# Stick-breaking scans over 640 columns in two pieces, and weight copies ranked 40 instructions higher

## The chip, the cores and the metric

The kernel runs on one core of a Trainium2 chip. The metric is the device time of one execution in microseconds (us). Engines: TensorE (PE) multiplies and transposes, VectorE (DVE) and ScalarE (ACT) evacuate and compute, GpSimd (POOL) does elementwise work on SBUF, SyncE (SP) issues nearly all DMAs.

## The reference, cut to what matters

One decoder layer over 1024 positions of width 1024, in float32. The projection `h @ w_in` feeds 8 heads of forgetting attention and 8 heads of stick-breaking attention (head width 64); then come group norms, an output projection, and a gated MLP with a causal convolution. The change concerns the stick-breaking heads, and one step that both kinds of heads share:

```python
mask = kpos[None, :] < qpos[:, None]
z = jnp.einsum('bhqd,bhkd->bhqk', qi, kf) * scale
log_beta = jax.nn.log_sigmoid(z)
log_one_minus = jnp.where(mask, jax.nn.log_sigmoid(-z), 0.0)
after = lax.cumsum(log_one_minus, axis=3, reverse=True) - log_one_minus
weights = jnp.where(mask, jnp.exp(log_beta + after), 0.0)
out = jnp.einsum('bhqk,bhkd->bhqd', weights, vf)
```

So a weight is sigmoid(z) times the product of sigmoid(-z) over all later keys before the query.

## The kernel before, in words

Queries are handled in blocks of 128 (`i` = 0 to 7); block `i` sees n = 128 (i + 1) keys, so its widest row has 128 to 1024 columns. Blocks go in groups of two (`g` = 0 to 3), in the order 0, 1, 3, 2, for one head after another: 8 forgetting heads, then 8 stick-breaking ones.

For a stick-breaking block, `score` (lines 455 to 501) multiplies q with the keys (lines 472, 473; keys come as a high and a low part), adds the mask (476), and lets ACT write sigmoid(-z) to `qi` and sigmoid(z) to `w` (486, 487), in up to two chunks. Then DVE runs one scan (line 499), backwards from column T - 1 = 1023 over n columns: a running product, in place. Column T of `qi` holds 1.0. POOL multiplies `w` with the scanned row, shifted by one column (line 500). There are two `qi` tiles and four `w` tiles.

`trans` (503 to 521) turns the weights of a group: PE transposes up to four 128x128 tiles into one PSUM bank `tp` (511; two banks), ACT copies the bank to `ph` (519), rounded to the matmul type, and DVE subtracts, `pl` = `tp` - `ph` (520), the low part. On the diagonal the tiles are `pth` and `ptl`, of 384 columns. `pv` (523 to 541) multiplies them with v: lines 531 (`ph`) and 532 (`pl`), into the bank `o`; then DVE folds `o` into `ot` (`tm`, 540 and 541).

Between these steps runs filler work that needs no attention result: projections of later heads (lines 164 to 166, 282 to 284, evacuated by lines 237 to 242 and 291 to 293), and in the last heads the output projection of the forgetting group, with `ogl` (624), `t` (657, 658) and its store (659). SP loads the next head's q, `kh`, `kl` and v (437 to 450).

The order on PE, DVE, ACT and POOL is made by a planner: it lays out the whole program by modelled times, and where several instructions of an engine are ready takes that with the lowest rank number, which is the place in the program. `tc.high_priority(offset=n)` gives the instructions inside a rank n places earlier (a negative n: later). Each engine then runs its list in order. SP's list is in program order. `GIVE = 60` is such an offset already, for POOL's weight splits. The forget gate's cumulated sum (line 334) is a scan in two chained pieces already.

Of the kernel before, what the change touches and what calls it, by code (L numbers as in the profile page):

```python
# [13 lines left out]
ALU = mybir.AluOpType  # L14
# [5 lines left out]
T = 1024  # L20
# [34 lines left out]
UA = 3  # L55

GIVE = 60

PARTS = ((0, 512), (512, 256), (768, 256))
NORM_AT = ((1, 3), (2, 3), (3, 0))  # L60
# [5 lines left out]
def f32(ap):  # L66
    return ap.bitcast(F32)
# [3 lines left out]
def layer(ctx, tc, xT, wqk, wv0, wv, wout, wup, wdn, cols, fbias, yT):  # L71
    nc = tc.nc
# [43 lines left out]
    class W:  # L116
# [16 lines left out]
        def split(self, upto):  # L133
# [4 lines left out]
            while self.done < upto:  # L138
                q = self.n // self.pieces
                sl = slice(self.done * q, (self.done + 1) * q)  # L140
                first = self.act or self.index < 2
                with tc.high_priority(offset=0 if first else -GIVE):
                    if first:
# [273 lines left out]
    def defer(n, f):  # L417
        pend.append([n, f])
# [36 lines left out]
    def score(p, hb, i, ws):  # L455
        fox = p < NFOX
        q, kh, kl, vt, fbt = heads[p, hb]
        n = (i + 1) * P
        w = pp.tile([P, T], F32, name="w")
        ws[i] = w  # L460
        m = None
        if not fox:
            if len(qi) < NQ:
                qi.append(own.tile([P, T + 1], F32, name=f"qi{len(qi)}"))
                nc.gpsimd.memset(qi[-1][:, T:T + 1], 1.0)
            qt = qi[count[0] % NQ]
            count[0] += 1
        for c0, cn in CHUNKS[i]:
            s = ps_s.tile([P, 512], F32, name="s")
            qb = q[:, i * P:(i + 1) * P]  # L470
            diag = c0 <= i * P < c0 + cn
            nc.tensor.matmul(s[:, :cn], qb, kh[:, c0:c0 + cn], start=True, stop=False)
            nc.tensor.matmul(s[:, :cn], qb, kl[:, c0:c0 + cn], start=False, stop=not diag)
            if diag:
                o = i * P - c0
                nc.tensor.matmul(s[:, o:o + P], identb, mask_f if fox else mask_s,  # L476
                                 start=False, stop=True)
            un = min(cn, n - c0)
            if fox:
                m2 = small.tile([P, 1], F32, name="m")  # L480
                nc.vector.tensor_tensor_reduce(  # L481
                    out=w[:, c0:c0 + un], in0=s[:, :un], in1=fbt[:, c0:c0 + un], scale=-1.0,
                    scalar=3.0e38 if m is None else m, op0=ALU.add, op1=ALU.min, accum_out=m2)
                m = m2
            else:
                act(qt[:, T - n + c0:T - n + c0 + un], s[:, :un], AF.Sigmoid, scale=-1.0)  # L486
                act(w[:, c0:c0 + un], s[:, :un], AF.Sigmoid)

        if fox:
            l = small.tile([P, 1], F32, name="l")  # L490
            act(w[:, :n], w[:, :n], AF.Exp, scale=-1.0, bias=m, accum_out=l)  # L491

            def rest():
                nc.vector.reciprocal(l, l)  # L494
                nc.gpsimd.tensor_scalar(w[:, :n], w[:, :n], l, 1.0, ALU.mult, ALU.mult)  # L495
        else:
            def rest():
                rev = slice(T - 1, T - n - 1 if n < T else None, -1)
                nc.vector.tensor_tensor_scan(qt[:, rev], qt[:, rev], qt[:, rev], 1.0, ALU.mult, ALU.bypass)  # L499
                nc.gpsimd.tensor_tensor(w[:, :n], w[:, :n], qt[:, T - n + 1:T + 1], ALU.mult)  # L500
        defer(0, rest)

    def trans(g, mm, ws, box):
        last = mm == g
        z = P if last else 0
        tp = ps_t.tile([P, 512], F32, name="tp")
        for a, kb in enumerate((2 * mm + 1, 2 * mm)):
            for b in range(2):
                if kb > 2 * g + b:
                    continue  # L510
                nc.tensor.transpose(tp[:, a * 256 + b * P:a * 256 + (b + 1) * P],  # L511
                                    ws[2 * g + b][:, kb * P:(kb + 1) * P], ident)
        if last:
            ph, pl = ptl[count[1] % 2]
            count[1] += 1
        else:
            ph = ptp.tile([P, 512], F32R, name="ph")
            pl = ptp.tile([P, 512], F32R, name="pl")
        nc.scalar.copy(ph[:, z:], tp[:, z:])  # L519
        nc.vector.tensor_tensor(pl[:, z:], tp[:, z:], f32(ph[:, z:]), ALU.subtract)  # L520
        box[mm] = (ph, pl)

    def pv(p, hb, g, mm, box):
# [20 lines left out]
    def finish(p):  # L544
# [3 lines left out]
        def go():  # L548
# [9 lines left out]
            eng = nc.vector if p == NPAIR - 1 else nc.gpsimd  # L558
            with tc.high_priority(offset=0 if p == NPAIR - 1 else -GIVE):
                for sl in (slice(0, 512), slice(512, T)):  # L560
# [12 lines left out]
    def attention_stream():  # L573
        hs = [(p, hb) for p in range(NPAIR) for hb in range(2)]
        prev = []
        yield 0, partial(load_v, 0, 0)
        for n, (p, hb) in enumerate(hs):
            ws = {}
            order = ORDER_LAST if n == len(hs) - 1 else ORDER
            for gi, g in enumerate(order):  # L580
                if gi == 1 and n + 1 < len(hs):
                    yield 0, partial(load_head, *hs[n + 1])
                    yield 0, partial(load_v, *hs[n + 1])
                for i in (2 * g, 2 * g + 1):
                    cost = 2 * sum(c for _, c in CHUNKS[i]) / 2400 + 0.06
                    yield cost, partial(score, p, hb, i, ws)
                yield from prev
                box = {}
                tr = [(TRC, partial(trans, g, mm, ws, box)) for mm in range(g + 1)]
                pvs = [(0.67 - TRC, partial(pv, p, hb, g, mm, box)) for mm in range(g + 1)]  # L590
                prev = tr[:LAG]
                for mm in range(g + 1):
                    prev.append(pvs[mm])
                    prev += tr[mm + LAG:mm + LAG + 1]
                if n == len(hs) - 1:
                    if gi == 1:
                        prev += [(0, partial(load_og, 4)), (0, partial(load_og, 5))]
                    if gi == 2:
                        prev += [(0, partial(load_og, 6))]
            if hb == 1:  # L600
                prev.append((0.4, partial(finish, p)))
        yield from prev
# [683 lines left out]
```

## Time and profile before

| | |
|---|---|
| median of 3 runs | 1420.33 us (1416.86 to 1420.97) |
| profiled execution | 1420.63 us |
| its span | 1418.8 us |
| PE busy in the span | 1306.7 us (92%) |
| DVE busy | 1113.8 us (79%) |
| ACT busy | 622.8 us (44%) |
| POOL busy | 759.5 us (54%) |
| scans of line 499 on DVE | 64, 104.0 us |
| copies of line 519 on ACT | 160 |
| subtractions of line 520 on DVE | 160 |

The span is what the profiler saw from the first to the last instruction; the execution's own time is a little longer. "Busy" is the time in which an engine worked on an instruction, not the time in which it set the end.

### The profile page before, as it was taken

The page shows a single profiled execution, that of the slowest core. Times are in us where ns is not written, and L with a number is a line of the kernel's source. Part 1 is how long each engine was busy: PE and PEld are TensorE (multiplying, and loading weights), DVE is VectorE, ACT ScalarE, POOL GpSimd, SP SyncE. Part 2 cuts the span into 40 slices and gives each one's busy share as a digit, 9 for nine tenths or more (in the row PEclk, how much of TensorE's full clock was granted, in tenths as well). Part 3 has the DMA queues.
Part 4 walks back from the last instruction along what each step waited for, and adds up shares of the span by engine and source line. Part 5 has one row for each costly group of instructions (what it writes and reads, how often), then busy time and mean ns, then how long its engine had stood idle before and what let it go on. Part 6 is the DMA issues. An engine that isn't in the chain of part 4 may idle for free.

```text
span 1418.8 us, 19128 instructions
## 1 busy us (share of the span) xinstructions
PE 1306.7 (92%) x6640; PEld 1074.8 (76%) x6640; DVE 1113.8 (79%) x1646; ACT 622.8 (44%) x1136; POOL 759.5 (54%) x664
## 2 busy tenths in 40 slices
PE   7899999999898887799889999999999988999895
PEld 6879878877787766678667788888888866878685
DVE  7346555655676678697999999999889899899987
ACT  6234434444454455354544444344343363344334
POOL 4254354444647584440005788887778864445413
PEclk9999999999999999999989999999999999999997
DMA  5656555544534455547512332233332265445313
GB/s 182 193 159 193 149 164 157 147 134 133 165 105 133 119 155 157 149 157 237 184 60 68 111 111 95 92 111 112 111 112 97 97 222 193 163 149 169 99 30 119
DMA packets 97233, 194.89 MB, mean 137 GB/s; under 512 B 8680, under 2 KB 35688, under 8 KB 97136
## 3 DMA queue, kind: packets, MB, share of 16 engines
q1 hardware_dynamic: 96272, 193.04, 43.5%
q8 instruction: 52, 0.85, 0.3%
q10 hardware_dynamic: 864, 0.64, 0.1%
q14 instruction: 45, 0.37, 0.1%
HBM read 132.79 MB, written 60.85 MB: 136 GB/s over the span
## 4 chain that ended last, share of the span: by engine, by line
PE 53%; DMA 17%; DVE 16%; POOL 6%; issue 4%; ACT 2%; SPq 2%; DVEq 0%; POOLq 0%; ACTq 0%
PE u L165 8%; PE u L166 8%; PE u L164 8%; PE pj L164 5%; PE pj L166 5%; PE pj L165 5%; DMA q<-qkd 4%; DVE qi L499 3%; DMA vd<-vs 2%; PE tp L511 2%; PE o L532 2%; DMA oraw<-od 2%; PE pj L282 1%; PE pj L284 1%; PE pj L283 1%
## 5 line engine op out<-in xcount | busy, mean ns | idle before, releaser
L886 POOL TENSOR_TENSOR s<-wraw 128x512 f32<-128x512 f32 (+1 forms) x32 | 52.7, 1647 | 210.7 <-DMA wraw<-in_wup_dram 145.5
L500 POOL TENSOR_TENSOR w<-w,qi 128x128 f32<-128x128 f32 (+3 forms) x64 | 94.2, 1482 | 79.9 <-DVE qi L499 41.8
L913 ACT CAST wh<-s 128x512 fp32r<-128x512 f32 (+1 forms) x136 | 79.4, 591 | 119.9 <-POOL s L887 68.7
L499 DVE TENSOR_TENSOR_SCAN qi<-qi 128x128 f32<-128x128 f32 (+3 forms) x64 | 104.0, 1633 | 27.7 <-ACT qi L486 24.9
L146 POOL TENSOR_SCALAR wh<-wraw 128x256 fp32r<-128x256 f32 (+1 forms) x104 | 51.3, 512 | 124.4 <-DMA wraw<-in_wv_dram 51.0
L511 PE MATMUL tp<-ident,w 128*128 128x128 f32 x576 | 94.4, 282 | 19.3 <-DVE pl L520 8.4
L164 PE MATMUL pj<-xh,wh 128*128 128x512 f32 x224 | 101.8, 454 | 3.2 <-DVE yf L298 3.2
L511 PEld LDWEIGHTS tp<-ident,w 128*128 128x128 f32 x576 | 71.1, 145 | 38.2 <-DVE pl L520 12.0
L915 POOL TENSOR_TENSOR wl<-wraw,wh 128x512 fp32r<-128x512 f32 x58 | 100.0, 1731 | 0.0
L520 DVE TENSOR_TENSOR pl<-tp,ph 128x512 fp32r<-128x512 f32 x96 | 65.0, 685 | 36.1 <-ACT ph L519 35.8
L166 PE MATMUL pj<-xh,wl 128*128 128x512 f32 x224 | 90.9, 406 | 0.0
L491 ACT ACTIVATE w<-w,m 128x128 f32<-128x128 f32 (+3 forms) x64 | 49.7, 776 | 92.5 <-DVE m L481 87.2
L165 PE MATMUL pj<-xl,wh 128*128 128x512 f32 x224 | 90.1, 402 | 0.0
L1012 DVE SCALAR_TENSOR_TENSOR tg<-ua,col,tg 128x1023 f32<-128x1023 f32 (+1 forms) x44 | 88.9, 2020 | 0.2 <-ACT tg L1010 0.2
L486 ACT ACTIVATE qi<-s 128x512 f32<-128x512 f32 (+2 forms) x96 | 47.5, 494 | 86.7 <-PE s L476 41.0
L913 ACT CAST wh<-wraw 128x512 fp32r<-128x512 f32 (+1 forms) x96 | 55.1, 590 | 67.6 <-DMA wraw<-in_wdn_dram 26.3
L495 POOL TENSOR_SCALAR w<-w,l 128x128 f32<-128x128 f32 (+3 forms) x64 | 47.9, 754 | 68.0 <-DVE l L494 35.1
L282 PE MATMUL pj<-wh,xh 128*128 128x256 f32 (+1 forms) x256 | 78.5, 307 | 1.5 <-DVE yf L298 1.5
L519 ACT CAST ph<-tp 128x512 fp32r<-128x512 f32 x96 | 55.9, 588 | 52.8 <-PE o L531 33.1
L915 POOL TENSOR_TENSOR wl<-s,wh 128x512 fp32r<-128x512 f32 x44 | 73.1, 1662 | 10.8 <-ACT wh L913 10.4
L148 POOL TENSOR_TENSOR wl<-wraw,wh 128x256 fp32r<-128x256 f32 (+1 forms) x104 | 78.0, 772 | 0.2
L1012 DVE SCALAR_TENSOR_TENSOR tv<-ub,col,tv 128x1023 f32<-128x1023 f32 (+1 forms) x44 | 73.9, 1680 | 2.3 <-ACT tv L1010 2.1
(366 smaller groups left out, 4508.6 us busy)
## 6 DMA issues: line engine op xcount, KB each, us to landing
wraw<-in_wup_dram SPq DMA_DIRECT2D x47, 512.0 KB, 3.7
st<-td SPq DMA_DIRECT2D x74, 256.0 KB, 3.9
qkd<-hl SPq DMA_DIRECT2D x32, 512.0 KB, 3.0
td<-tg SPq DMA_DIRECT2D x44, 256.0 KB, 2.3
vd<-vs SPq DMA_DIRECT2D x32, 256.0 KB, 4.5
q<-qkd SPq DMA_DIRECT2D x16, 512.0 KB
kh<-qkd SPq DMA_DIRECT2D x32, 256.0 KB, 17.0
kl<-qkd SPq DMA_DIRECT2D x32, 256.0 KB, 17.5
```

The lines of the kernel that those rows point to most:

```text
L148: eng.tensor_tensor(self.lo[:, sl], self.raw[:, sl], f32(self.hi[:, sl]), ALU.subtract)
L164: nc.tensor.matmul(ps, ah, bh, start=start, stop=False)
L165: nc.tensor.matmul(ps, ah, bl, start=False, stop=False)
L166: nc.tensor.matmul(ps, al, bh, start=False, stop=stop)
L282: nc.tensor.matmul(ps[:, :n], xh[k][:, sl], h, start=(k == 0), stop=False)
L499: nc.vector.tensor_tensor_scan(qt[:, rev], qt[:, rev], qt[:, rev], 1.0, ALU.mult, ALU.bypass)
L500: nc.gpsimd.tensor_tensor(w[:, :n], w[:, :n], qt[:, T - n + 1:T + 1], ALU.mult)
L511: nc.tensor.transpose(tp[:, a * 256 + b * P:a * 256 + (b + 1) * P], ws[2 * g + b][:, kb * P:(kb + 1) * P], ident)
L520: nc.vector.tensor_tensor(pl[:, z:], tp[:, z:], f32(ph[:, z:]), ALU.subtract)
L913: nc.scalar.copy(h[:, o:o + w], src)
L915: eng.tensor_tensor(l[:, o:o + w], src, f32(h[:, o:o + w]), ALU.subtract)
L1012: nc.vector.scalar_tensor_tensor(t[:, s:], us[:, :T - s], col[:, cw + tap:cw + tap + 1], t[:, s:], op0=ALU.mult, op1=ALU.add)
```

## The change

Two edits, in the functions printed above.

The scan of a block with n over 640 (blocks 5, 6 and 7) is made in two instructions: the last 512 columns, then the other n - 512 (256, 384 or 512). The second starts from the last value of the first, read from `qi`.

The copy to `ph` (or `pth`) on ACT and the subtraction to `pl` (or `ptl`) on DVE get a rank 40 places earlier, in all 16 heads.

```diff
 GIVE = 60
+
+SOON = 40
...
         else:
             def rest():
-                rev = slice(T - 1, T - n - 1 if n < T else None, -1)
-                nc.vector.tensor_tensor_scan(qt[:, rev], qt[:, rev], qt[:, rev], 1.0, ALU.mult, ALU.bypass)
+                last = 1.0
+                for a, b in ((T, T - 512), (T - 512, T - n)) if n > 640 else ((T, T - n),):
+                    rev = slice(a - 1, b - 1 if b else None, -1)
+                    nc.vector.tensor_tensor_scan(qt[:, rev], qt[:, rev], qt[:, rev], last, ALU.mult, ALU.bypass)
+                    last = qt[:, b:b + 1]
                 nc.gpsimd.tensor_tensor(w[:, :n], w[:, :n], qt[:, T - n + 1:T + 1], ALU.mult)
         defer(0, rest)
...
-        nc.scalar.copy(ph[:, z:], tp[:, z:])
-        nc.vector.tensor_tensor(pl[:, z:], tp[:, z:], f32(ph[:, z:]), ALU.subtract)
+        with tc.high_priority(offset=SOON):
+            nc.scalar.copy(ph[:, z:], tp[:, z:])
+            nc.vector.tensor_tensor(pl[:, z:], tp[:, z:], f32(ph[:, z:]), ALU.subtract)
         box[mm] = (ph, pl)
```

## Rows read from the trace of the kernel before

**Rows 1.** Stretches: start:end, length, busy PE, PEld, DVE, ACT, POOL, granted clock, DMA, GB/s.
```profile
98.00:345.00 247.00, 236.55 (x1529) 204.19 (x1529) 147.65 (x429) 108.17 (x234) 111.56 (x160) 0.99 0.54 155
345.00:645.00 300.00, 260.42 (x1520) 215.93 (x1520) 221.59 (x284) 147.25 (x312) 171.77 (x161) 0.94 0.48 140
```

**Rows 2.** Waits of PE from 345 to 645: total us, times, longest.
```profile
PE o L532 <- DVE pl L520: 12.1, 7, 3.2
PE tp L511 <- POOL w L500: 7.7, 5, 5.4
...
PE tp L511 <- DVE pl L520: 4.8, 3, 2.0
PE o L532 <- DVE ptl L520: 4.0, 6, 1.9
```

**Rows 3.** Timeline of one head: start, duration, instruction [idle before <-releaser].
```profile
401.44 1.78 POOL L500 TENSOR_TENSOR w<-w,qi 128x896 f32<-128x896 f32 x1 [3.11 <-DVE qi L499]
...
402.19 3.17 DVE L499 TENSOR_TENSOR_SCAN qi<-qi 128x1024 f32<-128x1024 f32 x1 [0.92 <-ACT qi L486]
...
403.03 0.59 ACT L519 CAST ph<-tp 128x512 fp32r<-128x512 f32 x1
...
405.39 0.61 DVE L293 SCALAR_TENSOR_TENSOR vs<-pj,rst,vs 128x128 fp32r<-128x128 f32 x2
...
405.92 0.68 DVE L520 TENSOR_TENSOR pl<-tp,ph 128x512 fp32r<-128x512 f32 x1
...
406.65 0.38 PE L532 MATMUL o<-pl,vt 128*128 128x256 f32 x1 [1.78 <-DVE pl L520]
```

**Rows 4.** Timeline: short scans of three widths.
```profile
413.44 1.76 DVE L499 TENSOR_TENSOR_SCAN qi<-qi 128x768 f32<-128x768 f32 x1 [0.87 <-ACT qi L486]
...
510.71 2.28 DVE L499 TENSOR_TENSOR_SCAN qi<-qi 128x1024 f32<-128x1024 f32 x1
...
611.37 1.21 DVE L499 TENSOR_TENSOR_SCAN qi<-qi 128x512 f32<-128x512 f32 x1
```

**Rows 5.** Timeline of PE: gaps that end with a low copy.
```profile
372.30 0.39 PE L532 MATMUL o<-pl,vt 128*128 128x256 f32 x1 [0.98 <-DVE pl L520]
...
442.47 0.39 PE L532 MATMUL o<-pl,vt 128*128 128x256 f32 x1 [2.21 <-DVE pl L520]
...
478.49 0.39 PE L532 MATMUL o<-pl,vt 128*128 128x256 f32 x1 [3.22 <-DVE pl L520]
...
621.57 0.38 PE L532 MATMUL o<-pl,vt 128*128 128x256 f32 x1 [0.93 <-DVE pl L520]
...
632.19 0.66 PE L511 MATMUL tp<-ident,w 128*128 128x128 f32 x4 [2.03 <-DVE pl L520]
```

**Rows 6.** Timeline of DVE ahead of the last of these.
```profile
630.28 1.25 DVE L624 SCALAR_TENSOR_TENSOR ogl<-oraw,col,ogh 128x1024 fp32r<-128x1024 f32 x1
...
631.46 0.68 DVE L520 TENSOR_TENSOR pl<-tp,ph 128x512 fp32r<-128x512 f32 x1
```

**Rows 7.** Timeline of PE: two other gaps late in the stretch.
```profile
549.41 0.35 PE L472 MATMUL s<-kh,q 128*128 128x256 f32 x1 [1.45 <-DMA kh<-qkd]
...
593.77 0.80 PE L164 MATMUL pj<-ogh,wh 128*128 128x512 f32 x1 [5.43 <-DVE t L657]
```

**Rows 8.** Timeline: one product on POOL and the transposes that read it.
```profile
443.37 2.00 POOL L500 TENSOR_TENSOR w<-w,qi 128x1024 f32<-128x1024 f32 x1
...
446.32 0.60 PE L511 MATMUL tp<-ident,w 128*128 128x128 f32 x4
```

**Rows 9.** Busy time by stretch, behind two of the gaps (columns as above).
```profile
406.60:412.60 6.00, 5.95 (x34) 5.71 (x35) 3.41 (x6) 2.52 (x7) 2.19 (x2) 0.72 0.37 126
442.40:448.40 6.00, 5.93 (x36) 5.15 (x37) 4.46 (x7) 4.05 (x10) 4.43 (x4) 1.00 0.33 126
```

**Rows 10.** Waits from 345 to 640, all engines: one row.
```profile
ACT ph L519 <- PE o L531: 21.1, 7, 10.3
```

**Rows 11.** Timeline of POOL: the product of another head's block 6.
```profile
369.48 3.75 POOL L500 TENSOR_TENSOR w<-w,qi 128x896 f32<-128x896 f32 x1
```

## The prediction

> **What bounds the kernel now.** I read the busy time by stretch first. In the forgetting-attention stretch (98 to 345 us) TensorE (PE) is busy 236.55 of 247.00 us, so nearly nothing is to be won there. In the stick-breaking stretch (345 to 645 us) it is busy 260.42 of 300.00 us at a mean granted clock of 0.94: 39.6 us are idle, and all scans of the change lie here [rows 1]. Then I read what PE waited for in this stretch. 20.9 us of the idle time end with a `pl` or `ptl` copy of line 520: 12.1 us in seven gaps before the second attention product (line 532), 4.8 us in three gaps before a transpose, 4.0 us in six gaps on `ptl`. POOL's product of line 500 ends another 7.7 us [rows 2].
>
> The timeline of one such gap shows why `pl` is late. The scan of 1024 columns starts at 402.19 and takes 3.17 us. `ph` is ready at 403.03 + 0.59 = 403.62, but VectorE (DVE) works in order: the scan, two `vs` evacuations, then `pl` at 405.92. PE, which needs `pl`, stands for 1.78 us until 406.65 [rows 3]. Of the seven gaps of 12.1 us I list five, each behind the 1024-column scan of a different head: 0.98, 1.78, 2.21, 3.22 and 0.93 us [rows 3, 5]. The same rows show what stretches a scan. A 1024-column scan can take 2.28 us [rows 4]; this one began while POOL's product (401.44 to 403.22) ran, and it ended 2.14 us after the product did. So it seems to have stood still until POOL was done.
>
> **What the split gives.** Each head has three scans over 640 columns (blocks 5, 6 and 7), and there are 8 stick-breaking heads: 24 scans become 48. A 512-column scan takes 1.21 us, a 1024 one 2.28, a 768 one 1.76 [rows 4]. Two pieces of 512 are 2.42 us, so a split costs about 0.15 us of DVE: 24 x 0.15 = 3.6 us. This is hidden: DVE is busy 221.59 of 300.00 us in the stretch [rows 1]; if that cover were gone, the 3.6 us would be the price. What comes back: after the first piece DVE can take `pl`, which is then 2.28 - 1.21 = 1.07 us earlier behind a 1024 scan and 1.76 - 1.21 = 0.55 us earlier behind a 768 one. A `pl` that outranks its neighbours by 40 also passes the small work that stood before it.
>
> Gap by gap, never more than the gap itself:
> - 372.30: the whole 0.98. 442.47: 1.07 of 2.21. 478.49: 1.07 of 3.22. 621.57: the whole 0.93 [rows 5].
> - 406.65: 1.07, and the first of the two `vs` evacuations and a part of the second, 0.53 (405.92 - 405.39), so 1.60 of 1.78 [rows 3].
> - The other two of the seven hold 12.1 - 9.1 = 3.0 us. I count them as nothing: some microseconds behind the one PE waits for the DMA of `kh` (549.41), behind the other for 5.43 us for an evacuation that a store holds up (593.77); arriving there earlier only lengthens those waits [rows 7].
> - The three gaps before a transpose hang on 768 scans: 0.55 each, and at 632.19 also the `ogl` of 1.25 us that stands ahead of `pl` [rows 5, 6]: 2 x 0.55 + 1.80 = 2.90.
> - The six `ptl` gaps stand behind 512 and shorter scans, which stay whole. Only the rank could help: between 0 and 4.0 us [rows 2]. I take 0, the nearest row being an undivided scan.
>
> Sum: 0.98 + 1.60 + 1.07 + 1.07 + 0.93 + 2.90 = 8.55 us.
>
> **What is late next.** The second piece now waits for `pl` (0.68 us) and often `ptl`, so the product of block 7 on POOL, and the transposes that read it, come about 1.3 us later, while PE arrives 1 us sooner. PE bears that where it has over 2.3 us between product and transpose. At one head the product ends at 443.37 + 2.00 = 445.37 and the transpose starts at 446.32, a margin of 0.95 [rows 8]: up to 1.4 us of a new wait. But POOL also gets its turn between the pieces, so it starts the product of block 6 sooner. I take 0.5 us for this head, nothing at the others, and keep -1.4 us each for the five heads (7 us) as the bad end.
>
> **The clock.** After the gap of 1.78 us PE ran the next 6 us at a mean granted clock of 0.72, part of the time thus at the lower of its two levels (1.2 and 2.4 GHz); after the longer one of 2.21 us it kept 1.00 [rows 9]. So a gap doesn't always cost clock. The first of these shrinks to 0.2 us; I count its 6 x 0.28 = 1.7 us as won, and no other.
>
> **The rank in the forgetting heads.** There is no scan, but `ph` and `pl` move up against the exponentials and minima. The most that could come back is the 10.45 us that PE stands idle there. The other way: 8 heads x 4 groups x one cast of 0.59 us [rows 3] = 19 us of delays, of which PE, idle 4% of the time, would feel 0.8. I take 0.
>
> No DMA and no step of SP is moved; the bytes stay.
>
> **Sum.** 8.55 - 0.5 + 1.7 = 9.75 us. The profiled execution took 1420.63 us (span 1418.8 and 1.83 around it), 0.3 above the median of the runs. 1420.63 - 9.75 = 1410.9, so 1411 us.
>
> **The rivals.**
> *A: the rank does more than the split.* Where `ph` is done before the 1024 scan starts, the planner can put `pl` ahead of the whole scan, and `ptl` ahead of the 512 ones. Then all 20.9 us go, and the clock's 1.7: 1420.6 - 22.6 = 1398. For it: the gap of 3.22 us is longer than any scan of 2.28, so something was ready long before. Against it: at 402.19 `ph` ended 1.4 us after the scan began [rows 3], and an order that keeps DVE idle for a copy is not what a rank gives. 0.12.
>
> *B: nothing reaches the end.* The copies stay where they are in DVE's order, or the time won falls into the next waits: POOL's product (7.7 us in five gaps now [rows 2]), loads, stores [rows 7]. 1420 us. For it: the longest of PE's waits in rows 7 ends with an evacuation behind a store. Against it: over half of PE's 39.6 idle us end with `pl` or `ptl` [rows 1, 2], and their cause is the order on one engine. 0.20.
>
> *C, slower: POOL slips in between the pieces.* The product of block 6 at 369.48 took 3.75 us where the same shape takes 1.78 [rows 3, 11]: it waited for the scan to end. If the scan is cut and the two pieces still stand together in DVE's order, the waiting product starts after the first piece, the second piece waits for its 1.78 us, and everything behind it on DVE (`pl`, `tm`, evacuations) is that much later. For five gaps (four 1024 scans and one 768 one) 5 x 1.78 = 8.9 us: 1429.5 us. It decides only where `pl` is not between the pieces and a POOL instruction waits at that moment. Against it: `pl` outranks the second piece and takes just that place, and it has only one SBUF operand. 0.10. The Trainium skill ("SBUF — State Buffer", section "Who interferes with whom") has this as a rule: a VectorE instruction with two SBUF inputs and a GpSimd instruction that reads SBUF exclude one another, and the later one waits for the whole of the earlier. The trace agrees in both directions (2.14 us after the product's end; 3.75 for 1.78 us).
>
> *D, slower: ScalarE (ACT) is held.* ACT waited 21.1 us, seven times, with a `ph` at its head whose buffer PE had not yet read out [rows 10]. A `ph` ranked higher can come to stand ahead of the next block's sigmoids; they wait with it, the score banks fill up and PE stops. 3.0 us (21.1 / 7) in each of 8 heads is 24 us, less the 9.75 won: 1435 us. It decides where the hold is longer than the filler products that PE has before its next score. Against it: PE waits for ACT hardly at all now. 0.06.
>
> **Chances and range.** Forecast 0.52, with its own range 1404 to 1417; A 0.12; B 0.20; C 0.10; D 0.06. Within 0.3% (4.3 us, what a measurement of this kernel can tell from no change) lie 0.08 of the forecast and 0.14 of B: 0.22. Faster: 0.44 + 0.12 + 0.02 = 0.58. Slower: C, D and 0.04 of B: 0.20. The range goes from A's 1398 to 1430, past C; it leaves out D and the tails.
>
> **What would show it.** Right: in DVE's timeline of each stick-breaking head, scan piece, `pl`, scan piece; the 12.1 and 4.8 us of PE's waits for `pl` down to some 5 and 2; the stretch after 345 shorter by about 10 us, with the forgetting stretch and everything behind 645 as long as before. A would show `pl` before the first piece and the `ptl` waits gone too. C would show second pieces of 2.5 us or more with a POOL product inside them. D would show PE waiting for ACT's sigmoids in scores. I am wrong if the waits for `pl` fall and POOL's product (line 500) takes their place as what PE's transposes wait for, or if the stretch from 98 to 345 changes by more than 4 us.

## The result and the profile after

The changed kernel took 1426.67 us (median of 5 runs, 1424.61 to 1430.04), the kernel before 1417.97 beside it (5 runs, 1415.24 to 1420.97): a ratio of 1.0064 [1.0048, 1.008], 8.7 us slower. The forecast was 1411. The likely case went the wrong way, and the signs that the prediction gave for rival C are in the profile after.

First the stretches, as in [rows 1].

```profile
98.00:345.00 247.00, 235.16 (x1527) 201.88 (x1526) 148.46 (x430) 108.14 (x233) 111.19 (x160) 1.00 0.54 156
345.00:645.00 300.00, 254.56 (x1463) 210.41 (x1462) 224.55 (x292) 143.34 (x307) 164.59 (x161) 0.93 0.46 136
```

The forgetting heads are as before (PE's first wait behind them ends at 343.85 us instead of 344.25). In the second stretch PE is busy for 5.86 us less, at a clock lower by 0.01. A stretch of fixed length hides how late the work ends, so the next rows go from 344 us to the first matmul of `u`, the product that follows all heads (655.76 us before, 665.42 after): one row of the kernel before, then one of the kernel after.

```profile
344.00:655.76 311.76, 271.20 (x1579) 225.01 (x1580) 227.86 (x298) 152.21 (x319) 171.77 (x161) 0.95 0.47 140
```

```profile
344.00:665.42 321.42, 274.82 (x1579) 227.35 (x1580) 241.00 (x322) 152.04 (x319) 164.59 (x161) 0.94 0.46 135
```

The head stretch is 9.66 us longer, the whole span 9.1 (1427.9 against 1418.8): it all happens here. DVE has 24 instructions more and 13.1 us more busy time. Of PE's 9.66 us, 6.0 are idle time (40.6 to 46.6, length less busy). PE's busy time grew by 3.6; by windows of 5 us, busy time times (1 - granted clock) went from 12.9 to 16.2, so 3.3 of those 3.6 are time at the lower clock level.

What PE waited for, from 345 to 655 us (answers to [rows 2]; before, that window gives the same figures as the rows there):

```profile
PE o L538 <- DVE pl L526: 14.5, 6, 3.8
PE tp L516 <- DVE pl L526: 8.7, 7, 2.8
PE tp L516 <- POOL w L505: 8.3, 7, 4.0
PE o L538 <- DVE ptl L526: 4.4, 7, 2.0
```

The waits for `pl` rose from 12.1 + 4.8 to 14.5 + 8.7: 6.3 us, about the whole of the added idle time. The change was to shorten just these.

The first stick-breaking head shows how (timeline of DVE, POOL and PE; it answers to the first of [rows 5], a gap of 0.98 us):

```profile
369.41 1.19 DVE L503 TENSOR_TENSOR_SCAN qi<-qi 128x512 f32<-128x512 f32 x1
...
369.66 2.52 POOL L505 TENSOR_TENSOR w<-w,qi 128x896 f32<-128x896 f32 x1 [0.98 <-DVE qi L503]
...
370.64 2.62 DVE L503 TENSOR_TENSOR_SCAN qi<-qi 128x512 f32<-128x512 f32 x1
...
373.18 0.66 DVE L526 TENSOR_TENSOR pl<-tp,ph 128x512 fp32r<-128x512 f32 x1
...
373.89 0.39 PE L538 MATMUL o<-pl,vt 128*128 128x256 f32 x1 [1.73 <-DVE pl L526]
```

The two pieces of the 1024-column scan follow one another, `pl` behind both. POOL's product of block 6 was issued at 369.66, during the first piece; it ended at 372.18. The second piece took 2.62 us, where the first took 1.19, and ended at 373.26, 1.08 us after the product. So POOL got in between and the second piece stood until POOL was done: a slip, in what follows. PE's gap is 1.73 instead of 0.98. In the third head it is worse (the four pieces of blocks 6 and 7 in one row, with two POOL instructions inside it; 2.21 before [rows 5]):

```profile
437.18 7.24 DVE L503 TENSOR_TENSOR_SCAN qi<-qi 128x512 f32<-128x512 f32 x4 [1.87 <-ACT qi L488]
...
437.63 2.21 POOL L244 TENSOR_TENSOR hl<-full,hl 128x512 fp32r<-128x512 f32 x1
...
440.83 2.51 POOL L505 TENSOR_TENSOR w<-w,qi 128x896 f32<-128x896 f32 x1 [0.99 <-DVE qi L503]
...
444.34 0.66 DVE L526 TENSOR_TENSOR pl<-tp,ph 128x512 fp32r<-128x512 f32 x1
...
445.06 0.58 PE L538 MATMUL o<-pl,vt 128*128 128x256 f32 x1 [3.83 <-DVE pl L526]
```

In DVE's timeline of the eight heads `pl` stands between the pieces of the 1024-column scan in none (between those of the 768-column scan it does in the third, seventh and eighth). In five heads (1, 2, 3, 5, 7) the pieces stand together ahead of it; in the sixth and eighth something else parts them, and POOL slips in there too. The sixth head:

```profile
548.48 2.51 POOL L505 TENSOR_TENSOR w<-w,qi 128x896 f32<-128x896 f32 x1 [4.79 <-DVE qi L503]
...
549.46 0.42 DVE L546 COPY tm<-o 64x256 f32<-64x256 f32 x1
549.91 2.17 DVE L503 TENSOR_TENSOR_SCAN qi<-qi 128x512 f32<-128x512 f32 x1
```

So block 6's product slips into the 1024-column scan in four heads, the first, third, sixth and eighth: second pieces of 2.62, 2.61, 2.17 and 2.01 us where undisturbed ones take 1.27 to 1.28, in all 4.3 us more. In the second, fourth and seventh head the product began before the first piece, which stood for it (2.34 to 2.52 us), as the whole scan did before. In the fourth `pl` stands ahead of both pieces, and there the gap of 3.22 us [rows 5] is gone, but a new one of 2.01 us appears, on `ptl`, which a POOL product made late:

```profile
477.95 0.69 DVE L526 TENSOR_TENSOR pl<-tp,ph 128x512 fp32r<-128x512 f32 x1
478.09 1.78 POOL L505 TENSOR_TENSOR w<-w,qi 128x896 f32<-128x896 f32 x1 [2.31 <-ACT pth L525]
478.56 2.39 DVE L503 TENSOR_TENSOR_SCAN qi<-qi 128x512 f32<-128x512 f32 x1
480.87 0.53 DVE L526 TENSOR_TENSOR ptl<-tp,pth 128x384 fp32r<-128x384 f32 x1
481.32 1.27 DVE L503 TENSOR_TENSOR_SCAN qi<-qi 128x512 f32<-128x512 f32 x1
481.45 0.38 PE L538 MATMUL o<-ptl,vt 128*128 128x256 f32 x1 [2.01 <-DVE ptl L526]
```

### The profile page after: what moved, and what is told of

Same layout as the page of the kernel before. It is cut to its first block, busy times and chain, and to the rows that moved or that the text cites. A ratio compares the mean times of both kernels' runs of the same rounds, so it can differ in the third digit from the quotient of the medians.

```text
span 1427.9 us, 19139 instructions
## 1 busy us (share of the span) xinstructions
PE 1311.8 (92%) x6640; PEld 1076.5 (75%) x6640; DVE 1123.9 (79%) x1670; ACT 622.9 (44%) x1136; POOL 751.1 (53%) x664
## 4 chain that ended last, share of the span: by engine, by line
PE 53%; DVE 18%; DMA 16%; POOL 5%; issue 4%; ACT 3%; SPq 1%; DVEq 0%; POOLq 0%; ACTq 0%
PE u L167 8%; PE u L168 8%; PE u L166 8%; PE pj L168 5%; PE pj L166 5%; PE pj L167 5%; DVE qi L503 3%; DMA kl<-qkd 2%; DMA kh<-qkd 2%; DMA q<-qkd 2%; DMA wraw<-in_wqk_dram 2%; PE tp L516 2%; PE o L538 2%; DMA st<-td 2%; DVE wl L921 1%
## 5 line engine op out<-in xcount | busy, mean ns | idle before, releaser
L503 DVE TENSOR_TENSOR_SCAN qi<-qi 128x512 f32<-128x512 f32 (+4 forms) x88 | 115.4, 1317 | 25.7 <-ACT qi L488 22.2
L505 POOL TENSOR_TENSOR w<-w,qi 128x128 f32<-128x128 f32 (+3 forms) x64 | 87.4, 1371 | 88.4 <-DVE qi L503 53.4
L150 POOL TENSOR_TENSOR wl<-wraw,wh 128x256 fp32r<-128x256 f32 (+1 forms) x104 | 82.9, 816 | 0.5
```

Of the source, the lines that this page charges most:

```text
L150: eng.tensor_tensor(self.lo[:, sl], self.raw[:, sl], f32(self.hi[:, sl]), ALU.subtract)
```

## The experiments

The theory was C (theory L in some expectations): a split opens a door for POOL, and the second piece pays a whole POOL instruction. The rivals: the rank does the harm; or the order of the whole plan decides, so that what is won or lost at one wait is made up at others, whatever POOL does between the pieces. Eleven kernels ran, in three groups (e1 to e4, e5 to e8, e9 to e11), each group with runs of the kernel before on its chip (1417.55, 1417.81, 1419.19 us).

The table sums up PE's time from 344 us to the first `u` matmul, made for each kernel as above: idle, lost to the lower clock, and the rest of its busy time. Each profile is one execution. The kernel before alone ranged from 1412.1 to 1425.0 us in these runs, at mean granted clocks of 0.975 to 0.964, and its profiled execution, 1420.63 us, lies above all its medians; so a few us of a difference in the columns idle and clock can belong to the execution. Differences in time are those of the medians; the ratios give up to 3 us more or less.

| kernel | median us, ratio to before | stretch | idle | clock | rest |
|---|---|---|---|---|---|
| before | | 311.8 | 40.6 | 12.9 | 258.3 |
| after | 1426.67, 1.0064 [1.0048, 1.008] | 321.4 | 46.6 | 16.2 | 258.6 |
| e1 split only | 1434.31, 1.011 [1.0092, 1.0127] | 325.2 | 47.1 | 19.8 | 258.3 |
| e2 rank only | 1416.2, 0.9985 [0.9972, 0.9999] | 307.2 | 40.2 | 8.6 | 258.4 |
| e3 tied, block 7 | 1426.97, 1.0065 [1.0051, 1.008] | 316.9 | 44.3 | 13.4 | 259.2 |
| e4 tied, blocks 5, 7 | 1420.67, 1.0019 [1.0008, 1.0029] | 310.9 | 38.6 | 11.7 | 260.6 |
| e5 no products, whole | 1414.31, 0.9965 [0.995, 0.998] | 305.8 | 38.1 | 8.9 | 258.8 |
| e6 no products, split | 1416.49, 0.9986 [0.9965, 1.0006] | 307.7 | 40.9 | 9.4 | 257.4 |
| e7 held, whole | 1430.89, 1.0081 [1.0057, 1.0106] | 321.0 | 42.2 | 21.4 | 257.5 |
| e8 held, split | 1434.76, 1.0122 [1.0089, 1.0155] | 326.8 | 47.3 | 18.3 | 261.2 |
| e9 e4 with the rank | 1420.69, 1.0016 [1.0002, 1.0031] | 312.1 | 43.2 | 9.0 | 259.9 |
| e10 split block 7 | 1428.87, 1.0088 [1.0061, 1.0115] | 321.1 | 46.0 | 19.7 | 255.4 |
| e11 split blocks 5, 6 | 1421.13, 1.0025 [1.0009, 1.0042] | 313.4 | 43.5 | 12.2 | 257.7 |

**e1 and e2: each half alone.** e1 is the kernel after without `with tc.high_priority(offset=SOON)`, e2 the kernel before with it.

> The scans over 640 columns in two pieces, the ranks as before the change. Theory C (the pieces stand together in DVE's order, and a POOL instruction that waits for the first piece runs between them, so DVE stands still for it): as slow as the changed kernel, 1424 to 1430 us, 0.4 to 0.8% over before, with PE's waits for pl before line 532's products from 345 us on at 13 us or more. Rival R (the rank is what costs): within 0.3% of before. Rival O (only the cost of 24 more instructions, 3.6 us at most): 0 to 0.25% over before.

> Whole scans, the copies ranked 40 higher. Theory C: the rank finds nothing to change where pl waits, within 0.3% of before (1414 to 1422 us), PE's waits for pl within 2 us of before. Rival R: slower by 0.4 to 0.8%, as the changed kernel. Rival A of the prediction (the rank puts pl ahead of whole scans): faster by over 0.5%.

The split alone costs 16.8 us, more than expected; the rank alone does next to nothing (-1.4 us, at the edge of its interval). Together they cost 8.7, so with the split in place the rank takes back half of its price. That the rank does the harm is ruled out. PE's waits for `pl` in e1:

```profile
PE o L537 <- DVE pl L525: 17.7, 7, 3.8
PE tp L516 <- DVE pl L525: 9.7, 7, 2.8
```

That is 10.5 us more than before, while the idle time grew by 6.5 (other waits shrank: the one on the evacuation `t` from 6.5 to 2.7 us, and those on `kh` and `kl`, 2.8 us, went) and the clock took 6.9. The clock's share can be seen behind one gap: in e1 the first head's gap is 2.00 us instead of 0.98, and behind it PE runs 10 us without a pause at little over the lower of its two levels (1.2 and 2.4 GHz). Three windows of e1:

```profile
370.00:375.00 5.00, 3.00 (x15) 2.48 (x14) 4.82 (x6) 0.93 (x2) 3.75 (x2) 0.84 0.37 142
375.00:380.00 5.00, 5.00 (x25) 4.91 (x25) 1.33 (x4) 3.08 (x7) 1.31 (x2) 0.50 0.34 124
380.00:385.00 5.00, 5.00 (x25) 4.71 (x24) 3.21 (x7) 2.92 (x5) 1.32 (x1) 0.53 0.00 0
```

From 375 to 385 us the kernel before had a clock of 1.00 and got through 88 matmuls; e1 shows 50.

**e3 and e4: `pl` put between the pieces by force.** The second piece starts from a value made of the first piece's last column and of 0.0 times a column of the last low copy, so it can't start before that copy (in e3's trace `ptl`, which follows `pl`):

```diff
+                scan(T, T - 512, 1.0)
+                def second():
+                    lk = small.tile([P, 1], F32, name="lk")
+                    nc.vector.scalar_tensor_tensor(lk, f32(low[0][:, 511:512]), 0.0, qt[:, T - 512:T - 511],
+                                                   op0=ALU.mult, op1=ALU.add)
+                    scan(T - 512, T - n, lk)
+                    end()
+                defer(ticks, second)
```

`end` is POOL's product, `low[0]` the last low copy. e3 does this for block 7 (`ticks` 1), e4 for block 5 too (`ticks` 0); all other scans stay whole.

> No rank; only the 1024-column scan is split, and its second piece is made to need the last copy (ptl) of the group in flight, through one 128x1 instruction of some 0.2 us, so that pl and ptl stand between the pieces. Theory C: pl is then 1.1 us or more earlier in each head, PE's 12.1 us of waits for pl before line 532's products fall to 4 to 7 us, and the kernel is 4 to 9 us faster than before (0.3 to 0.65%); a POOL product that runs meanwhile costs nothing. Rival O: 0 to 0.2% slower than before, since the split costs and the place of pl does not matter. Rival P (the product of block 7, now about 1.5 us later, becomes what PE waits for): the waits for pl fall as in C, those for POOL's product grow by as much, same time as before.

> As e3, and also the 768-column scan is split 512 + 256, its second piece tied behind the first pl of the group in flight. Theory C: another 0 to 2 us faster than e3, PE's 4.8 us of waits for pl before transposes at 2 to 3 us. Rival P: slower than e3 by 0 to 4 us, the product of block 5 being later too.

This is the nearest test of my forecast proper, and it failed too. In e3 `pl` stands where I wanted it, and the waits before the second product fell from 12.1 to 5.1 us, as the sum had it. The time went up by 9.4 us all the same. PE's waits in e3:

```profile
PE tp L531 <- DVE pl L540: 9.3, 7, 2.7
PE tp L531 <- POOL w L506: 7.5, 6, 5.2
PE o L553 <- DVE ptl L540: 5.7, 7, 1.9
PE o L553 <- DVE pl L540: 5.1, 5, 2.3
PE pj L164 <- DVE t L678: 4.6, 1, 4.6
PE s L473 <- DMA kh<-qkd: 3.4, 1, 3.4
PE s L474 <- DMA kl<-qkd: 2.5, 2, 1.4
```

What went at one wait came back at the next: at the transposes 4.8 to 9.3, at `ptl` 4.0 to 5.7, at the loads of `kh` and `kl` 2.8 to 5.9. In all PE was idle 44.3 us, 3.7 more than before. DVE's timeline shows one reason that is the experiment's own: the second piece came 2.3 us behind `pl`, not 0.7, with `ptl`, which it was tied to, an evacuation and `tm` ahead of it, so the product was later than in my sum:

```profile
370.36 1.78 DVE L503 TENSOR_TENSOR_SCAN qi<-qi 128x512 f32<-128x512 f32 x1
372.07 0.66 DVE L540 TENSOR_TENSOR pl<-tp,ph 128x512 fp32r<-128x512 f32 x1
...
374.37 1.27 DVE L503 TENSOR_TENSOR_SCAN qi<-qi,lk 128x512 f32<-128x512 f32 x1
```

e4 cost only 3.1 us, with 6.1 us of waits for `pl` before transposes where 2 to 3 were expected; why one tied scan more makes it 6 us better than e3 I can't say.

**e5 and e6: the products of blocks 5 to 7 left out.** In both `if n <= 640:` stands ahead of POOL's product, so block 4's product and POOL's `hl` subtraction still run beside scans; e6 has the split of the kernel after, without the rank.

> The kernel before, leaving out POOL's product of line 500 for blocks 5, 6 and 7 (their weights are then the bare sigmoids). It is the base for e6: whole scans, no product that can stop them. PE no longer waits for these products; 1400 to 1418 us.

> The scans split as in e1 and the same products left out as in e5; to be read against e5. Theory L (the split costs because POOL's product, waiting for the first piece, stops the second): e6 minus e5 is 0 to 5 us, where e1 minus before was 17 us. Rival S (the split costs by itself or by another order on the engines): e6 minus e5 is 10 to 17 us.

With no product to slip in, the split costs 2.2 us (1416.49 against 1414.31, with intervals that overlap) and not 16.8. The scans tell the same, grouped by shape on DVE from 345 to 665 us. The 512-column pieces and scans in e1, then in e6:

```profile
L503 DVE TENSOR_TENSOR_SCAN qi<-qi 128x512 f32<-128x512 f32 x40 | 64.0, 1600 | 16.0 <-ACT qi L488 15.4
```

```profile
L503 DVE TENSOR_TENSOR_SCAN qi<-qi 128x512 f32<-128x512 f32 x40 | 57.9, 1448 | 15.8 <-ACT qi L488 15.3
```

And the 1024-column scans, left whole, before and in e5:

```profile
L499 DVE TENSOR_TENSOR_SCAN qi<-qi 128x1024 f32<-128x1024 f32 x8 | 23.9, 2983 | 1.5 <-ACT qi L486 1.4
```

```profile
L499 DVE TENSOR_TENSOR_SCAN qi<-qi 128x1024 f32<-128x1024 f32 x8 | 19.9, 2484 | 1.5 <-ACT qi L486 1.4
```

2983 ns with the products, 2484 without: 0.5 us of a whole scan is standing for these products. The rule of the Trainium skill that the prediction gave to C ("SBUF — State Buffer", section "Who interferes with whom") agrees with this and with the 2.62 us above. Leaving the products out takes a load off POOL as well, so this pair bounds the mechanism rather than isolates it.

**e7 and e8: the products kept, but held back.** The products of blocks 4 and 6 are issued only after the next block's scan, tied to it by a one-column instruction on DVE:

```diff
+                while held:
+                    ow, oend = held.pop()
+                    nc.vector.scalar_tensor_tensor(ow[:, 0:1], qt[:, T - n:T - n + 1], 0.0, ow[:, 0:1],
+                                                   op0=ALU.mult, op1=ALU.add)
+                    oend()
```

> The kernel before, whole scans; the products of blocks 4 and 6 are held back until the scan of the next block is done (by a 128x1 instruction on DVE that writes a weight column back after that scan), so that they cannot run ahead of it and stop it. Theory L: the 1024-column scans lose their 0.9 to 1.3 us of standing still in four or five heads, PE's waits for pl before line 532's products fall from 12.1 to 7 to 9 us; the time is 0 to 4 us less than before. Rival P (the later product of block 6 makes PE's transposes wait): 2 to 6 us slower than before.

> The scans split as in e1, with the products of blocks 4 and 6 held back as in e7, so that no product can run between the pieces of blocks 5 and 7. Theory L: at least 6 us faster than e1 (1428 us or less); the pieces of 512 stand 2.4 to 2.6 us together. Rival S: as slow as e1 (1430 to 1437), or slower by the held products.

I had hoped for a faster kernel and got one 13.1 us slower. The whole scans are free of these products (1024 columns: mean 2482 ns). PE's waits in e7 are on `ptl` as much as on `pl` now, many and short (4.0 us in six gaps before [rows 2]):

```profile
PE o L544 <- DVE pl L532: 11.4, 7, 2.7
PE o L544 <- DVE ptl L532: 11.2, 11, 1.9
```

Idle time grew by only 1.6 us, time at the lower clock by 8.5. Against this base, with the products out of the way, the split costs 3.9 us (1434.76 against 1430.89, intervals overlapping), again much less than 16.8. But e8 itself missed what I expected, 1428 us or less: it is as slow as e1, rival S's figure, though no product slips into its 1024-column scans. The two pairs agree with the slip as most of the split's price; they don't prove it, since e7 shows that a changed order with whole scans can cost 13.1 us.

**e9 to e11: which scan, and a last try.** e9 is e4 with the rank. e10 and e11 are e1 with other conditions: `n > 896` (block 7 alone) and `640 < n < 1024` (blocks 5 and 6).

> The tied pieces of e4 together with the rank of the change. Theory L with what e3 showed (each copy that comes earlier lets PE reach the next wait earlier; the rank then helps at the other waits): at or below e2 (rank alone, 0.15% under before) and e4 (0.2% over), 1410 to 1418 us, PE's idle time from 344 us to its first matmul of the next stage at 36 to 40 us. Rival N (a new plan each time, whose waits differ by chance): anywhere from 1408 to 1428 us, with idle time and lost clock not following the waits for pl.

> Only the 1024-column scan in two pieces, not tied, no rank. Theory L: the pieces stand together and POOL's product of block 6 runs between them in the heads where that product becomes ready as the scan starts (three or four of eight, 1.8 us each): 4 to 10 us over before, waits for pl before line 532's products 15 us or more. Rival S (cost per added instruction): 0 to 2 us over before.

> Only the scans of 768 and 896 columns in two pieces, not tied, no rank. Theory L: POOL's hl subtraction or product of block 4 runs between them, 3 to 8 us over before, and the waits for pl before transposes (behind the 768 scan) grow from 4.8 to 7 us or more. With e10 it adds up to e1's 17 us within 5 us. Rival S: 0 to 3 us over before.

e9 took 1420.69 us, where theory L had 1410 to 1418, with 43.2 us of idle time, where it had 36 to 40. So the rank adds nothing to the tied order, and rival N, that each new plan shifts the waits by chance, is not excluded. e10 costs 9.7 us, so the split of the 1024-column scan carries more of the price: PE's waits for `pl` before the second product are 15.5 us, against 12.1. But one wait for a load of `kh` also grew there, from 1.4 to 6.4 us, and the clock took 6.8 more; how these hang on the slip I can't show. The first head shows the slip again, longer: two pieces in 4.44 us around a product of 2.69.

```profile
366.60 4.44 DVE L503 TENSOR_TENSOR_SCAN qi<-qi 128x512 f32<-128x512 f32 x2
...
367.27 2.69 POOL L505 TENSOR_TENSOR w<-w,qi 128x896 f32<-128x896 f32 x1
```

The product ends at 369.96, the second piece at 371.04, 1.08 us later, as in the kernel after. e11 costs 1.9 us by the medians, less than the 3 to 8 expected, and 3.5 by its ratio; the waits before transposes rose from 4.8 to 8.0 us as expected. By the medians the two halves make 11.6 us and the whole 16.8; by the ratios they make 16.0 (12.5 and 3.5) and the whole 15.6. So no gap between the halves and the whole is shown.

## Why the prediction was wrong

**The step that failed** is "after the first piece DVE can take `pl`". It could: `ph` was ready at 368.81 us in the first head (368.16 + 0.65), before even the first piece of 1024 columns ran. But DVE runs a list that was made beforehand, and in that list `pl` stands between the pieces of a 1024 scan in no head. So the 1.07 us per gap never came about, and PE's waits for `pl` grew by 6.3 us. I argued against C that `pl` outranks the second piece and takes just that place; a rank only decides among instructions that the planner holds to be ready at that moment. That its modelled `ph` comes too late is inferred from the list, not tried.

**C was given too little chance, and its price came near in part by luck.** Its condition (pieces together, a POOL instruction waiting) was in the prediction, and 1429.5 us lies 2.8 from the median. But its price was five slips of 1.78 us each. The four slips into 1024-column scans come to 4.3 us on DVE, and the whole scans had stood for POOL before, so all pieces of these scans took 28.0 us against 23.9. What the stretch lost is 6.0 us of idle time and 3.3 of clock. From one head's scan of block 6 to the next one's, the first, third and sixth head, with a slip, took 1.7, 2.7 and 4.7 us more than before, and the second and seventh, without, 0.7 and 0.8 less; but the eighth, with one, lost nothing up to the first `u` matmul. e5 against e6 and e7 against e8 agree with the mechanism.

**The second assumption, that a shorter gap reaches the end, failed in e3.** With `pl` between the pieces the gaps shrank by 7.0 us, as sized, and the time rose by 9.4 us. I had let time won at two of seven gaps be swallowed by loads and stores [rows 7], and took the others as clear. This is rival B's mechanism, though not quite the prediction's sign: in e3 the transposes' new waits are on `pl` (4.8 to 9.3 us), and those on POOL's product stayed (7.7 and 7.5). e3's late second piece is part of it, so e3 doesn't show what the split as forecast would have done.

**The split's own cost** was put at 3.6 us of DVE, hidden. DVE's busy time to the first `u` matmul rose by 13.1 us, and it was not hidden. Without products to slip in, e6 and e8 leave 2 to 4 us of device time (3 to 6 by the ratios).

**The clock** went the other way: 1.7 us won was forecast, 3.3 lost was measured, no more than single executions differ by. The step behind it failed as well. In the second head the gap did not shrink but grew, from 1.78 to 2.01 us, and yet the 6 us behind it ran at 1.00 instead of 0.72 [rows 9]; behind the third head's gap of 3.83 us the clock was at its lower level, where it had been 1.00 [rows 9]:

```profile
408.52 0.39 PE L538 MATMUL o<-pl,vt 128*128 128x256 f32 x1 [2.01 <-DVE pl L526]
```

```profile
408.50:414.50 6.00, 5.98 (x47) 5.75 (x48) 4.30 (x8) 4.02 (x10) 2.48 (x2) 1.00 0.36 125
445.10:451.10 6.00, 6.00 (x21) 5.33 (x22) 2.70 (x4) 2.07 (x6) 2.02 (x2) 0.50 0.33 124
```

**Right** were the forgetting heads (0 forecast, 0.4 us measured), A's rejection (though the 3.22 us that spoke for A stand behind a scan of 3.60 us, not of 2.28), and that ACT is not held (D): PE waits 1.2 us for `ph` and 1.3 for sigmoids in the whole stretch. Not all of the six `ptl` gaps stand behind short scans, as the prediction read them: one, 0.53 us at 622.83, follows a 1024-column scan.

**Open:** how the split's 16.8 us divide between slips and the changed plan behind them (no run keeps the plan and takes away only the slip); e3 against e4; and a split with `pl` directly ahead of the second piece and no slip, which no run here has.

## What to carry to other kernels

Before cutting a long instruction so that a short one can pass, look in the engine's ordered list for whether it will pass, and look which other engine waits at the cut: if the two exclude one another, the cut hands the place over. A gap of PE that closes only counts when the next wait behind it hangs on something else. Read PE's lost clock beside its idle time; in the profiles of the slower orders here (the kernel after, e1, e7, e10) it was a third to nine tenths of what the stretch lost.

## What the runs showed of the hardware

The scan with POOL's product issued during its first piece is a strict turn-taking: second pieces ended 1.08 us after the product in two kernels (372.18 to 373.26, 369.96 to 371.04), whether the product itself took 2.52 or 2.69 us. In the kernel after, from 344 us on, 39 scans and pieces took over 0.05 us longer than undisturbed ones of their width. Each of them ended at a time after a POOL instruction's end that goes by its width, whichever instruction that was: 0.27 to 0.28 us at 128 columns, 0.53 to 0.55 at 256, 0.81 to 0.82 at 384, 1.07 to 1.08 at 512 and 1.35 at 640. And the granted clock can cost more than the idle time that goes with it: in e7's profile 8.5 us more than before against 1.6.
